# Where the low parts of split activation blocks stand in VectorE's queue

## The chip, the cores and the metric

The kernel runs on one core of a Trainium2 chip. The metric is device time in microseconds (us) of one execution, the median of several runs. A core has TensorE (PE in the profile; its weight loads are shown apart, as PEld), VectorE (DVE), ScalarE (ACT), GpSimd (POOL) and SyncE (SP), each with a queue of its own that is worked off in program order, and 16 DMA engines that the queues feed.

## The reference

One layer of a hybrid decoder for 512 prompt tokens and 8 × 4 new tokens of running sequences, 544 tokens in all, D_MODEL = 2048, float32:

```python
h = rmsnorm(x); proj = h @ w_in                 # q,k,v of 8 heads; q,k,v,gates of 4 GLA heads
gla_part = rmsnorm(gla(...)) * silu(gg)         # gated linear attention, 1024 wide
att_part = rmsnorm(dilated_attention(...))      # 1024 wide
x = x + concatenate([gla_part, att_part]) @ w_out
h = rmsnorm(x)
x = x + square(relu(h @ w_up)) @ w_down         # 4 * D_MODEL wide
y = rmsnorm(x)
```

New keys and values and the states of the linear attention are outputs too.

## The kernel before

**Data.** Activations lie transposed: a tile holds 128 features by 544 tokens, and the matmuls take the tokens in two halves of 272. One core does everything.

**Split operands.** TensorE multiplies in a rounded format (fp32r). So that float32 accuracy is kept, each operand is given as two: a high part, which is the value rounded to fp32r (ACT copies it), and a low part, which is the value minus the high part (DVE subtracts). A product is then three matmuls: high weight × high activation, high × low, low × high. Weights are split by `split_w` (line 231): its high tiles are called wh (whP in the MLP), its low tiles wl (wlP). Activations are split by `put_x` (line 331): ACT writes the high part, and the next instruction that DVE gets is the subtraction that waits for it. Activation tiles are all called b in the profile, whatever they hold, so a DVE row "TENSOR_TENSOR b<-b,b 128x544 fp32r" is the low part of an activation.

**Stages**, in order of time in the profiled execution:

1. Input projection (up to about 720 us), with the attention and the GLA heads worked in between as generators, a step at a time (`bg`). The last of them, `att_norm` (line 663), scales the eight heads of attention (one DVE instruction each, SCALAR_TENSOR_TENSOR with nw) and splits them into the operands Y[0..7].
2. Output projection (about 725 to 927 us), 16 column blocks × two halves of the inner dimension, each a `slot_main` (line 1056) of 48 matmuls. In its first half, `put_go` (line 1126) splits one GLA block per slot, and `state_gen` (line 1224) updates the GLA states of the new tokens (loads and stores on POOL's DMA queue, "b<-vs" and "gs<-b"; DVE adds). In its second half, `evac_wo` (line 1197) puts small pieces of work into a list, `post`: scale the new x, square it, sum, and then form the operands of the MLP (up_b2, up_b1, up_ta, up_ta2, up_tb, up_tb2; `two`, line 1145, and `one` do the splitting).
3. MLP up (about 927 to 1612 us). The product is a 2 × 2 block scheme with seven products (P1 to P7) in place of eight, in 32 pairs of column blocks p = 0..31; a unit is half of one product, 12 matmuls. DVE forms sums of weight quarters (`add_w`) and splits them. What comes out of a pair is evacuated, squared, and mixed again by the pieces of `hidden_ops` (line 1378) into operands for the down product, which are split (`spill_two`, line 1372) and stored to memory ("hs<-b"; for the last four pairs "hl<-b").
4. MLP down (about 1612 us to the end), in seven groups with the operands loaded back ("b<-hs") by `h_some`, then a last group and the final norm.

**What sets the order.** `run` (line 1332) issues a unit: it prepares the weights of the unit three places ahead (ACT high part, DVE sums and low part), then takes one or two pieces from `post`, then issues the 12 matmuls, then the evacuation. `slot_main` does alike: half of the matmuls, one to three pieces from `post`, a step of the generators, the other matmuls. Each engine works its queue in this order.

**Storage.** A tile is taken by `alloc` and given back by `rel`; a slot that was given back is used for a new tile, whose first writer then waits for the last reader of the old one.

Of the kernel before, what the change touches and what calls it, by code (L numbers as in the profile page):

```python
# [6 lines left out]
F32 = mybir.dt.float32  # L7
# [116 lines left out]
def _body(ctx, nc, tc, A):  # L124
# [201 lines left out]
    def mpair():  # L326
        i = mrot[0]
        mrot[0] ^= 1
        return mbank[2 * i], mbank[2 * i + 1]

    def put_x(dst_h, dst_l, src, scale=None):
        if scale is None:
# [330 lines left out]
    def att_norm():  # L663
        ss = None
        for h in range(8):
            while ("p", h) not in att_done or ("s", h) not in att_done:
                yield "wait"
            t = alloc()
            S.activation(t, AO[h], AF.Square)
            if ss is None:  # L670
                ss = t
            else:
                G.tensor_add(ss, ss, t)
                rel(t)
            yield
        while len(bfree) < 2:
            yield "wait"
        b0, b1 = balloc(), balloc()
        r = alloc()
        rms_r(r, [ss], 1024, (b0, b1))  # L680
        brel(b0, b1)
        rel(ss)
        yield
        for h in range(8):
            while room() < 6:
                yield "wait"
            V.scalar_tensor_tensor(AO[h], AO[h], nw[:, 48 + h:49 + h], r, op0=OP.mult, op1=OP.mult)
            a, b = alloc(R32), alloc(R32)
            put_x(a, b, AO[h])
            rel(AO[h])  # L690
            Y[h] = (a, b)
            if h % 2:
                yield
        rel(r)
        att_fin[0] = True

# [359 lines left out]
    def slot_main(i, pb, xs_, c0, first, last, evac=None, nbg=1, hs=(0, 1)):  # L1056
        begin()
        load_to(i + NRAW + 1)
        prep_to(uidx[i] + AHEAD)
        h, l = wops(i)  # L1060
        for q in range(2):
            clk["P"] = max(clk["P"], spl[i, q])
            for c in range(4 * q, 4 * q + 4):
                xh, xl = xs_[c0 + c]
                mm(pb, h(c), xh, first and c == 0, False, hs)
                mm(pb, h(c), xl, False, False, hs)
            for _ in range(1 + (len(post) > 1) + (len(post) > 4)):
                if post:
                    post.pop(0)()
            if q or BG2:  # L1070
                bg(nbg)
            for c in range(4 * q, 4 * q + 4):
                mm(pb, l(c), xs_[c0 + c][0], False, last and c == 7, hs)
            if q == 0:
                prep_to(uidx[i] + AHEAD + 1)
        if evac is not None:
            evac(pb)
        slot[0] += 1
# [46 lines left out]

    def put_go(n):
        a, b = alloc(R32), alloc(R32)
        put_x(a, b, GO[n])
        rel(GO[n])
        Y[8 + n] = (a, b)  # L1130

    xr = {}
# [9 lines left out]
    xa = {}  # L1142
    xtiles = {k: [] for k in ("a2", "ta", "tb", "b1")}

    def two(op, xt, key, src, where):

        h, l = alloc(R32), alloc(R32)
        put_x(h, l, src)
        xtiles[key] += [h, l]
        for hf, k in enumerate(where):  # L1150
            op[k][xt] = (half(h, hf), half(l, hf))

    def one(op, j, src):
        t = alloc(R32)
        put_x(half(t, 0), half(t, 1), src)
        xtiles["b1"].append(t)
        op["P1"][j] = (half(t, 0), half(t, 1))

# [26 lines left out]

    def up_tb2(j):
        tb = mixed.pop((j, 1))
        two(XU, j, "tb", tb, ("P6", "P4"))
        rel(tb)

    def evac_att(nb):
        def f(pb):
# [122 lines left out]
    def product(key, ops, k, blocks, ps, start, stop):  # L1315
        def mm_():
            n = len(blocks)
            for j in blocks:
                while ops[k][j] is None or len(ops[k][j]) < 2:
                    (post if ops is XU else hq).pop(0)()  # L1320
            for w, o in ((whm, 0), (whm, 1), (wlm, 0)):
                for c, j in enumerate(blocks):
                    P.matmul(ps, w[key][:, c, :], ops[k][j][o], start=start and w is whm and o == 0 and c == 0,
                             stop=stop and w is wlm and c == n - 1, skip_group_check=True)
        return mm_
# [6 lines left out]
    def run(us):  # L1332
        for u in us:
            due = [f for s, f in later_u if s <= unit_no[0]]
            later_u[:] = [(s, f) for s, f in later_u if s > unit_no[0]]
            for f in due:
                f()
            prep_to(FIRST + u.step + 3)
            if u.before:
                u.before()  # L1340
            for _ in range(1 + (len(post) > 6)):
                if post:
                    post.pop(0)()
            u.mm()
            if u.after:
                u.after()
            unit_no[0] += 1
# [23 lines left out]

    def spill_two(src, dst, i):
        h, l = alloc(R32), alloc(R32)
        put_x(h, l, src)
        spill(h, dst[i])
        spill(l, dst[i + 1])

    def hidden_ops(p):
        g, j = p // 4, p % 4
        a1, a2 = hid.pop((p, 0)), hid.pop((p, 1))  # L1380
        if g == 7:
            def put(i, a):
                spill_two(a, A["hl"][2 * j + i], 0)
                rel(a)
            post.extend([lambda: V.tensor_mul(a1, a1, rr["sq"]), lambda: V.tensor_mul(a2, a2, rr["sq"]),
                         lambda: put(0, a1), lambda: put(1, a2)])
            return
        dst = A["hs"][g, j]
        m = {}

        def mix_a():
            ta = m["a"] = alloc()
            V.tensor_sub(half(ta, 0), half(a1, 1), half(a1, 0))
            V.tensor_sub(half(ta, 1), half(a1, 1), half(a2, 1))

        def first():
            t = alloc(R32)
            put_x(half(t, 0), half(t, 1), half(a1, 0))
            rel(a1)
            spill(t, dst[6])  # L1400

        def mix_b():
            tb = m["b"] = alloc()
            V.tensor_sub(half(tb, 0), half(a2, 1), half(m["a"], 0))
            V.tensor_sub(half(tb, 1), half(tb, 0), half(a2, 0))

        def put_a():
            spill_two(m["a"], dst, 2)
            rel(m["a"])

        def put_2():
            spill_two(a2, dst, 0)
            rel(a2)

        def put_b():
            spill_two(m["b"], dst, 4)
            rel(m["b"])

        post.extend([mix_a, first, mix_b, put_a, put_2, put_b])

# [348 lines left out]
    for s, (nb, hf) in enumerate(wo_seq):  # L1769
        if s == 16:  # L1770
            drain(lambda: all(n in GO for n in range(8)), gens)
            go_some(8)
            rel(GW["a"], GW["w"])
            for c in range(8):
                rel(*Y[c])
        state_step(2 if s < 16 else 1)
# [61 lines left out]
    for nb in range(16):  # L1838
# [3 lines left out]
        else:  # L1842
            final_out(1, nb)
        out_dma(1, nb, (nc.sync, nc.scalar)[nb % 2])
    assert not later and not later_u and not post


def shape_consts():
# [111 lines left out]
```

## Time and profile before

| | |
|---|---|
| median of 3 runs | 2325.3 us (2323.55 to 2328.4) |
| the profiled execution: its time | 2323.29 us |
| the profiled execution: span from the first to the last instruction | 2321.5 us |
| PE busy | 2277.4 us, 98% of the span |
| DVE busy | 1963.5 us, 85% |
| ACT busy | 1115.3 us, 48% |
| POOL busy | 126.7 us, 5% |
| chain of work that ended last | PE 86%, DVE 7%, DMA 4%, ACT 2% |

All instructions that go through the kernel's helper carry line 96, so groups are told apart by tile and shape. Matmuls are pipelined and their ends are modelled, so "busy" hides short waits; how many matmuls fall into a stretch of time tells more. A bracket behind a row, "[0.72 <-ACT b L96]", is the time that the engine sat idle before it and what ended that. A row that merges several instructions has their number behind an x.

### The profile page before, as it was taken

How to read it: one execution, taken by the hardware profiler on the slowest of the kernel's cores; microseconds unless marked ns; L12 is line 12 of the kernel's file. 1: busy time of each engine (PE TensorE's matmuls, PEld its weight loads, DVE VectorE, ACT ScalarE, POOL GpSimd, SP SyncE). 2: the span in 40 equal slices, each digit the busy share in tenths (PEclk: the TensorE clock that was granted, in tenths of full speed). 3: DMA queues.
4: the chain of work that ended last, by engine and by line, in shares of the span. 5: the costliest groups of instructions: out<-in, count | busy, mean ns of one | idle time of the engine just before them, and what ended most of it. 6: DMA issues, size and time to landing. Idle time of an engine off the chain costs nothing.

```text
span 2321.5 us, 47246 instructions
## 1 busy us (share of the span) xinstructions
PE 2277.4 (98%) x17960; PEld 2247.7 (97%) x17960; DVE 1963.5 (85%) x4343; ACT 1115.3 (48%) x2133; POOL 126.7 (5%) x182
## 2 busy tenths in 40 slices
PE   8999999999999999999999999999999999999997
PEld 8999999999989999999999999999999999999997
DVE  7888877889878987888888888887788888888995
ACT  5333343333345345666666666655444444444465
POOL 3000010000012630000000000000000000000000
PEclk9999999999999999999999999999999999999999
DMA  6777865645735974365566556667755664664564
GB/s 228 265 266 240 287 227 189 219 144 186 242 104 173 349 259 162 112 207 180 186 199 203 177 188 205 197 198 255 266 175 169 217 208 150 217 222 154 170 214 149
DMA packets 168191, 473.43 MB, mean 204 GB/s; under 512 B 20091, under 2 KB 29307, under 8 KB 167964
## 3 DMA queue, kind: packets, MB, share of 16 engines
q1 hardware_dynamic: 157340, 439.67, 56.7%
q0 software_dynamic: 9472, 29.63, 3.6%
q8 instruction: 141, 2.31, 0.4%
q10 hardware_dynamic: 1152, 1.11, 0.1%
q14 instruction: 86, 0.70, 0.1%
HBM read 393.07 MB, written 77.27 MB: 203 GB/s over the span
## 4 chain that ended last, share of the span: by engine, by line
PE 86%; DVE 7%; DMA 4%; ACT 2%; issue 1%; POOL 0%; SPq 0%; DVEq 0%; ACTq 0%
PE bank L96 86%; DVE b L96 5%; DMA b<-vs 2%; ACT b L96 1%; DVE wlP L96 1%; DMA b<-xT 1%; DMA b<-hs 1%; DVE wl L96 1%; ACT whP L96 0%; DMA b<-win 0%; DMA raw<-win 0%; DVE AT L96 0%; ACT wh L96 0%; DVE kv L96 0%; POOL b L96 0%
## 5 line engine op out<-in xcount | busy, mean ns | idle before, releaser
L96 PE MATMUL bank<-b,whP 128*128 128x272 f32 x6720 | 980.4, 288 | 7.5 <-ACT b L96 3.6
L96 PEld LDWEIGHTS bank<-b,whP 128*128 128x128 f32 x6720 | 895.5, 188 | 10.4 <-ACT whP L96 4.4
L96 PE MATMUL bank<-b,wlP 128*128 128x272 f32 x3360 | 561.0, 289 | 2.1 <-DVE wlP L96 2.1
L96 PE MATMUL bank<-b,wh 128*128 128x272 f32 x3904 | 529.9, 288 | 0.3 <-DVE b L96 0.3
L96 PEld LDWEIGHTS bank<-b,wh 128*128 128x128 f32 x3904 | 505.3, 188 | 0.5 <-DVE b L96 0.5
L96 PEld LDWEIGHTS bank<-b,wlP 128*128 128x128 f32 x3360 | 472.9, 188 | 6.6 <-DVE wlP L96 3.4
L96 ACT ACTIVATE whP<-b 128x512 fp32r<-128x512 f32 x480 | 299.3, 627 | 255.7 <-DVE b L96 198.4
L96 ACT ACTIVATE b<-b 128x544 fp32r<-128x544 f32 (+6 forms) x485 | 274.6, 572 | 277.3 <-DVE b L96 245.7
L96 DVE TENSOR_TENSOR wlP<-b,whP 128x512 fp32r<-128x512 f32 x480 | 328.9, 686 | 17.0 <-ACT whP L96 16.5
L96 DVE TENSOR_TENSOR b<-b,b 128x272 f32<-128x272 f32 (+8 forms) x574 | 274.7, 498 | 35.8 <-ACT b L96 31.6
L96 PE MATMUL bank<-b,wl 128*128 128x272 f32 x1952 | 297.8, 295 | 2.7 <-DVE wl L96 2.6
L96 PEld LDWEIGHTS bank<-b,wl 128*128 128x128 f32 x1952 | 261.6, 189 | 9.8 <-issue 4.4
L96 ACT ACTIVATE b<-bank 128x272 f32<-128x272 f32 (+4 forms) x247 | 98.0, 409 | 316.8 <-PE bank L96 293.4
L96 DVE TENSOR_TENSOR b<-b,bank 128x272 f32<-128x272 f32 x388 | 167.3, 433 | 58.4 <-PE bank L96 57.9
L96 DVE TENSOR_TENSOR wl<-raw,wh 128x512 fp32r<-128x512 f32 x244 | 167.0, 692 | 54.7 <-PE bank L96 30.9
L96 ACT ACTIVATE wh<-raw 128x512 fp32r<-128x512 f32 x244 | 149.4, 623 | 128.3 <-PE bank L96 116.0
L96 DVE TENSOR_TENSOR wlP<-mraw,whP 128x512 fp32r<-128x512 f32 x206 | 140.8, 687 | 47.5 <-ACT whP L96 39.1
L96 PE MATMUL bank<-b,b 128*128 128x272 f32 (+5 forms) x968 | 143.1, 304 | 6.3 <-ACT b L96 6.3
L96 ACT ACTIVATE whP<-mraw 128x512 fp32r<-128x512 f32 x206 | 124.0, 621 | 41.4 <-PE bank L96 40.6
L96 POOL TENSOR_TENSOR b<-b,b 128x544 f32<-128x544 f32 (+2 forms) x26 | 36.4, 1403 | 1885.7 <-ACT b L96 1773.3
L96 DVE TENSOR_TENSOR wlP<-raw,whP 128x512 fp32r<-128x512 f32 x154 | 105.4, 687 | 34.5 <-ACT whP L96 28.3
L96 PEld LDWEIGHTS bank<-b,b 128*128 128x128 f32 (+2 forms) x968 | 119.3, 180 | 12.3 <-ACT b L96 6.6
(92 smaller groups left out, 1668.5 us busy)
## 6 DMA issues: line engine op xcount, KB each, us to landing
hs<-b SPq DMA_DIRECT2D x196, 272.0 KB, 6.0
b<-hs SPq DMA_DIRECT2D x196, 272.0 KB, 4.9
raw<-win SPq DMA_DIRECT2D x90, 512.0 KB, 4.2
mraw<-wdn SPq DMA_DIRECT2D x82, 512.0 KB, 3.6
kv<-kcg SPq DMA_DIRECT2D x64, 640.0 KB, 5.3
kv<-vcg SPq DMA_DIRECT2D x64, 640.0 KB, 5.4
mraw<-wup SPq DMA_DIRECT2D x74, 512.0 KB, 4.1
raw<-wdn SPq DMA_DIRECT2D x62, 512.0 KB, 3.7
```

Source lines behind the costliest of these rows:

```text
L96: return f(*a, **k)
```

## The change

A new helper `put_lag` takes the place of `put_x` for the operands of the output projection, of the MLP's first product and of its second. ACT's high part is issued where it was; the DVE subtraction (with the giving back of the source tile) goes into a list `lows`. `flush` issues what is in the list. It is called ahead of each piece taken from `post` (`piece`), ahead of the pieces of a slot and of a unit, in `att_norm` behind the scaling of the next head, at the end of `att_norm` and of the first half of the output projection, and, for the operands of the MLP's first product (tag "X"), ahead of the matmuls of a unit. In the last four pairs of MLP up an empty piece stands ahead of the two splits. The arithmetic is the same.

```diff
+    lows = []
+    def flush(tag=None):
+        for x in [x for x in lows if tag in (None, x[0])]:
+            lows.remove(x)
+            x[1]()
+    def piece():
+        flush()
+        post.pop(0)()
+    def put_lag(tag, dst_h, dst_l, src, *done):
+        S.activation(dst_h, src, AF.Copy)
+        def low():
+            V.tensor_sub(dst_l, src, dst_h.bitcast(F32))
+            rel(*done)
+        lows.append((tag, low))
...
@@ att_norm
             V.scalar_tensor_tensor(AO[h], AO[h], nw[:, 48 + h:49 + h], r, op0=OP.mult, op1=OP.mult)
             a, b = alloc(R32), alloc(R32)
-            put_x(a, b, AO[h])
-            rel(AO[h])
+            flush()
+            put_lag("Y", a, b, AO[h], AO[h])
...
+        flush()
         rel(r)
@@ slot_main
+            flush()
             for _ in range(1 + (len(post) > 1) + (len(post) > 4)):
                 if post:
-                    post.pop(0)()
+                    piece()
@@ put_go
-        put_x(a, b, GO[n])
-        rel(GO[n])
+        put_lag("Y", a, b, GO[n], GO[n])
@@ two (and one alike)
-        put_x(h, l, src)
+        put_lag("X", h, l, src, *done)
@@ product
                 while ops[k][j] is None or len(ops[k][j]) < 2:
-                    (post if ops is XU else hq).pop(0)()
+                    if ops is XU:
+                        piece()
+                    else:
+                        hq.pop(0)()
+            if ops is XU:
+                flush("X")
@@ run
+            flush()
             for _ in range(1 + (len(post) > 6)):
                 if post:
-                    post.pop(0)()
+                    piece()
@@ spill_two (and first alike)
-        put_x(h, l, src)
+        put_lag("H", h, l, src, src)
@@ hidden_ops, g == 7
-            post.extend([lambda: V.tensor_mul(a1, a1, rr["sq"]), lambda: V.tensor_mul(a2, a2, rr["sq"]),
+            post.extend([lambda: V.tensor_mul(a1, a1, rr["sq"]), lambda: V.tensor_mul(a2, a2, rr["sq"]), lambda: None,
                          lambda: put(0, a1), lambda: put(1, a2)])
```

PE's and POOL's queues have the same instructions in the same order before and after. DVE's differ at many places, ACT's and SP's only near the end of MLP up. Three places follow, as they stand in the queues (- before, + after).

DVE, in `att_norm`, heads 0 to 3: each SCALAR_TENSOR_TENSOR scales one head, the TENSOR_TENSOR with two b behind it is that head's low part, and wl is the low part of an input weight.

```order
 L96 SCALAR_TENSOR_TENSOR b_1091<-b_1091,nw,b_8209 128x544
+L96 SCALAR_TENSOR_TENSOR b_1445<-b_1445,nw,b_8209 128x544
 L96 TENSOR_TENSOR b_8311<-b_1091,b_8310 128x544
-L96 SCALAR_TENSOR_TENSOR b_1445<-b_1445,nw,b_8209 128x544
-L96 TENSOR_TENSOR b_8316<-b_1445,b_8315 128x544
-L96 TENSOR_TENSOR wl_0_8330<-raw_8113,wh_0_8277 128x512
+L96 TENSOR_TENSOR wl_0_8329<-raw_8113,wh_0_8277 128x512
+L96 TENSOR_TENSOR b_8315<-b_1445,b_8314 128x544
 L96 SCALAR_TENSOR_TENSOR b_1799<-b_1799,nw,b_8209 128x544
```

The second head's scaling now stands ahead of the first head's low part, and the weight's low part ahead of the second head's.

DVE, in MLP up, pair p = 2, the stretch from the units of P6 to those of P3 and P7: wlP are the low parts of the summed weights (quarters 0 and 1), "b<-mraw,mraw" a weight sum, the TENSOR_TENSOR of 128x544 the low parts of the three mixed blocks of the pair before.

```order
 L96 TENSOR_TENSOR wlP_2_0_11845<-b_11795,whP_2_0_11843 128x512
+L96 TENSOR_TENSOR b_11863<-mraw_11330,mraw_11418 128x512
+L96 TENSOR_TENSOR wlP_2_1_11867<-b_11815,whP_2_1_11865 128x512
 L96 TENSOR_TENSOR b_11848<-b_11776,b_11847 128x544
-L96 TENSOR_TENSOR b_11864<-mraw_11330,mraw_11418 128x512
-L96 TENSOR_TENSOR wlP_2_1_11868<-b_11816,whP_2_1_11866 128x512
+L96 TENSOR_TENSOR wlP_2_0_11893<-b_11841,whP_2_0_11891 128x512
 L96 TENSOR_TENSOR b_11871<-b_11657,b_11870 128x544
-L96 TENSOR_TENSOR wlP_2_0_11894<-b_11841,whP_2_0_11892 128x512
+L96 TENSOR_TENSOR wlP_2_1_11915<-b_11863,whP_2_1_11913 128x512
 L96 TENSOR_TENSOR b_11897<-b_11822,b_11896 128x544
```

Each of the three low parts stands one weight later; the weight of quarter 1 has moved ahead of the first of them.

ACT, in MLP up, pair p = 29, while the two results of pair 28 are split: whP are high parts of weights, "b<-bank" copies out of the accumulators, "b<-b" of 128x544 the high parts of the two results.

```order
 L96 ACTIVATE whP_29_1_19706<-b_19660 128x512
-L96 ACTIVATE b_19710<-b_19385 128x544
-L96 ACTIVATE b_19726<-bank_73 128x272
-L96 ACTIVATE whP_29_0_19734<-b_19685 128x512
-L96 ACTIVATE b_19738<-b_19561 128x544
-L96 ACTIVATE whP_29_1_19756<-b_19704 128x512
+L96 ACTIVATE b_19722<-bank_73 128x272
+L96 ACTIVATE whP_29_0_19730<-b_19685 128x512
+L96 ACTIVATE b_19734<-b_19385 128x544
+L96 ACTIVATE whP_29_1_19751<-b_19704 128x512
+L96 ACTIVATE b_19756<-b_19561 128x544
```

Both high parts stand one unit later, the copy out of the accumulator and the weight of quarter 0 ahead of the first.

More of the change, by code (lines that the diff above doesn't have):

```diff
@@ L1143, in _body, with two @@
     xtiles = {k: [] for k in ("a2", "ta", "tb", "b1")}
-    def two(op, xt, key, src, where):
+    def two(op, xt, key, src, where, *done):
         h, l = alloc(R32), alloc(R32)
-        put_x(h, l, src)
+        put_lag("X", h, l, src, *done)
         xtiles[key] += [h, l]
@@ L1154, in one @@
         t = alloc(R32)
-        put_x(half(t, 0), half(t, 1), src)
+        put_lag("X", half(t, 0), half(t, 1), src)
         xtiles["b1"].append(t)
@@ L1187, in up_tb2 @@
         tb = mixed.pop((j, 1))
-        two(XU, j, "tb", tb, ("P6", "P4"))
-        rel(tb)
+        two(XU, j, "tb", tb, ("P6", "P4"), tb)
     def evac_att(nb):
@@ L1383, in put @@
                 spill_two(a, A["hl"][2 * j + i], 0)
-                rel(a)
-            post.extend([lambda: V.tensor_mul(a1, a1, rr["sq"]), lambda: V.tensor_mul(a2, a2, rr["sq"]),
+            post.extend([lambda: V.tensor_mul(a1, a1, rr["sq"]), lambda: V.tensor_mul(a2, a2, rr["sq"]), lambda: None,
                          lambda: put(0, a1), lambda: put(1, a2)])
@@ L1397, in first @@
             t = alloc(R32)
-            put_x(half(t, 0), half(t, 1), half(a1, 0))
-            rel(a1)
+            put_lag("H", half(t, 0), half(t, 1), half(a1, 0), a1)
             spill(t, dst[6])
@@ L1408, in put_a @@
             spill_two(m["a"], dst, 2)
-            rel(m["a"])
         def put_2():
             spill_two(a2, dst, 0)
-            rel(a2)
         def put_b():
             spill_two(m["b"], dst, 4)
-            rel(m["b"])
         post.extend([mix_a, first, mix_b, put_a, put_2, put_b])
@@ L1773, in _body @@
             rel(GW["a"], GW["w"])
+            flush()
             for c in range(8):
@@ L1844, in _body @@
         out_dma(1, nb, (nc.sync, nc.scalar)[nb % 2])
-    assert not later and not later_u and not post
+    assert not later and not later_u and not post and not lows
 def shape_consts():
```

## Prediction

> **What bounds the kernel now.** I read the page's busy shares first, then the stretches of time, then who waits in those that lose time.
>
> ```profile
> PE 2277.4 (98%) x17960; PEld 2247.7 (97%) x17960; DVE 1963.5 (85%) x4343; ACT 1115.3 (48%) x2133; POOL 126.7 (5%) x182
> PE 86%; DVE 7%; DMA 4%; ACT 2%; issue 1%; POOL 0%; SPq 0%; DVEq 0%; ACTq 0%
> ```
>
> TensorE sets the time: it is 86% of the chain that ended last. DVE is in that chain with 7%, so moving DVE's work can pay only where PE waits. Busy time hides short waits; the number of matmuls in a stretch does not. The view of stretches (span from:to, its length, then busy time with the number of instructions for PE, PEld, DVE, ACT, POOL, then the granted clock, DMA share, GB/s):
>
> ```profile
> 714.00:726.00 12.00, 8.66 (x56) 7.98 (x55) 9.11 (x16) 6.07 (x13) 6.36 (x12) 0.86 0.75 263
> 754.00:780.00 26.00, 26.00 (x210) 26.00 (x209) 25.14 (x54) 10.33 (x20) 16.73 (x32) 1.00 0.96 347
> 780.00:816.00 36.00, 33.33 (x258) 32.23 (x257) 31.26 (x66) 10.31 (x20) 21.70 (x41) 1.00 0.97 353
> 924.00:936.00 12.00, 8.41 (x57) 8.22 (x56) 8.45 (x16) 6.75 (x12) 1.08 (x2) 0.86 0.12 48
> 968.00:992.00 24.00, 22.66 (x174) 21.85 (x172) 22.39 (x44) 14.21 (x29) 0.00 (x0) 1.00 0.52 168
> 992.00:1552.00 560.00, 559.98 (x4439) 556.79 (x4440) 491.96 (x870) 353.54 (x687) 0.00 (x0) 1.00 0.61 194
> 1552.00:1612.00 60.00, 57.24 (x441) 55.26 (x440) 48.58 (x80) 33.14 (x64) 0.00 (x0) 1.00 0.67 219
> 1612.00:1626.00 14.00, 12.17 (x93) 11.61 (x93) 11.09 (x19) 8.57 (x17) 0.00 (x0) 1.00 0.98 367
> 1626.00:2146.00 520.00, 520.00 (x4153) 520.00 (x4154) 452.09 (x861) 220.44 (x377) 0.00 (x0) 1.00 0.59 197
> ```
>
> MLP down (1626:2146) runs without waits: 520/4153 = 0.1252 us per matmul. By that price the others lose: 714:726 5.0 us (12 − 56 × 0.1252); 780:816 3.7; 924:936 4.9; 968:992 2.2; 992:1552 4.2; 1552:1612 4.8; 1612:1626 2.4. The change can reach at most about these 27 us, 1.2% of the time. I go through them in order.
>
> **A, 714:726, the split of the attention heads.** From the timeline (start, length, engine):
>
> ```profile
> 704.47 0.78 DVE L96 SCALAR_TENSOR_TENSOR b<-b,nw,b 128x544 f32<-128x544 f32 x1
> 705.28 0.66 ACT L96 ACTIVATE b<-b 128x544 fp32r<-128x544 f32 x1 [5.01 <-DVE b L96]
> 705.97 0.73 DVE L96 TENSOR_TENSOR b<-b,b 128x544 fp32r<-128x544 f32 x1 [0.72 <-ACT b L96]
> 709.43 0.78 DVE L96 SCALAR_TENSOR_TENSOR b<-b,nw,b 128x544 f32<-128x544 f32 x1
> 713.02 0.61 ACT L96 ACTIVATE wh<-raw 128x512 fp32r<-128x512 f32 x1
> 719.98 0.72 DVE L96 TENSOR_TENSOR b<-b,b 128x544 f32<-128x544 f32 x1
> 720.75 2.18 PE L96 MATMUL bank<-b,ones 128*128 128x272 f32 x4 [3.34 <-DVE b L96]
> ```
>
> For each head DVE scales, stands idle 0.72 us for ACT's high part, and subtracts. Three pairs of heads stand ahead of the sum at 719.98 that the matmul with ones waits for, and PE sits idle 3.34 us. A pair takes 709.43 − 704.47 = 4.96 us. In the new order the second scaling fills the first wait, and the second high part runs under the first low part. What is left is the weight's low part, which waits for the weight's high part, on ACT behind the second head's (0.66 + 0.61 us, less the low part's 0.64 beside it, as from 1032.44 to the next start at 1033.08 in C's rows: about 0.6 idle). The pair then takes 0.75 + 0.75 + 0.03 + 0.64 + 0.6 + 0.6 + 0.64 = 4.0 us, 0.95 less. Two pairs give 1.9 us; in the third, two evacuations stand between, cover both waits and give 0.7. That is 2.6 of PE's 3.34 us, the rest stays. Bounds: 0.7 (only the third pair pays, if the weights wait for PE) and 3.34.
>
> The row has a second price: the granted clock is 0.86 over these 12 us. At half clock that is 3.4 us, and of these PE works some 2.6 (from 720.75), which costs 1.3 us. A wait of 0.7 us in place of 3.3 should not bring that on. [...] A gives 2.6 + 1.3 = **3.9 us**, between 0.7 and 4.6.
>
> Does it come through? In 754:816 the DMA engines are 96 to 97% busy with the GLA states, and a chain of loads leads there:
>
> ```profile
> 742.26 0.16 DVE b L96
> 753.99 7.62 DMA b<-vs
> 805.85 5.70 DMA b<-vs
> ```
>
> The chain begins behind a DVE evacuation at 742.26, which itself waits for PE, and the DMA share of 714:726 is 0.75. So that work starts earlier by as much as PE does, and the stretch moves as a whole. Inside it DVE has 25.14 us of work in 26, no wait for ACT to remove. I take 0 for it; bounds −1 and +1 (one weight per slot comes a low part's 0.6 us earlier; or DMA meets other traffic).
>
> **B, 924:936, the first block of MLP up.**
>
> ```profile
> 924.32 0.69 DVE L96 TENSOR_TENSOR wlP<-mraw,whP 128x512 fp32r<-128x512 f32 x1 [0.34 <-issue]
> 926.79 0.73 DVE L96 TENSOR_TENSOR b<-b,b 128x544 fp32r<-128x544 f32 x1 [0.73 <-ACT b L96]
> 931.12 0.73 DVE L96 TENSOR_TENSOR b<-b,b 128x544 fp32r<-128x544 f32 x1 [0.72 <-ACT b L96]
> 931.76 0.78 DVE L96 TENSOR_TENSOR b<-bank,b 128x272 f32<-128x272 f32 x2
> 932.31 0.95 PEld L96 LDWEIGHTS bank<-b,whP 128*128 128x128 f32 x4 [3.78 <-ACT b L96]
> ```
>
> PE's wait of 3.78 us ends as the evacuation at 931.76 frees the bank. Of the two waits ahead of it the second stays: three pieces are taken in that slot, so its low part falls back in front of the evacuation. The first (0.73) goes, but a low part that stood ahead of 924.32 now stands behind that weight, which waits anyway (0.34, "issue"), and adds its 0.64. I take **0.1 us**, between −0.6 and 1.4 (the half clock gone too). **968:992** is a chain of evacuations, activations and weights, in which one low part moves behind the evacuation that ACT waits for; of 2.2 us I take a low part's 0.64, **0.6 us**, between 0 and 1.5.
>
> **C, 992:1552, the steady part of MLP up.** A pair of blocks is 14 units of 12 matmuls, 168; 4439/168 = 26.4 pairs, so 4.2 us are 0.16 us per pair. The timeline shows it, once per pair:
>
> ```profile
> 1032.44 0.72 DVE L96 TENSOR_TENSOR b<-b,b 128x544 fp32r<-128x544 f32 x1
> 1033.08 0.69 DVE L96 TENSOR_TENSOR b<-mraw,raw 128x512 f32<-128x512 f32 x1
> 1033.68 0.69 DVE L96 TENSOR_TENSOR wlP<-b,whP 128x512 fp32r<-128x512 f32 x1
> 1032.74 0.56 PEld L96 LDWEIGHTS bank<-b,wlP 128*128 128x128 f32 x4
> 1033.24 1.06 PEld L96 LDWEIGHTS bank<-b,whP 128*128 128x128 f32 x8
> 1034.42 0.55 PEld L96 LDWEIGHTS bank<-b,wlP 128*128 128x128 f32 x4
> ```
>
> A load of wlP should follow that of whP by 1.0 us; here it is 1.18, because DVE ends the weight at 1034.37. The low part at 1032.44 is the instruction that moves behind it. So the weight ends 0.64 earlier, 0.46 before PE asks. The two weights after it also have one low part less ahead of them, and the evacuation at the end has all three ahead as before. The removed wait does not come back elsewhere: DVE works 491.96 of 560 us. The stores of the low parts keep their place on SP, three units behind, 4.5 us against a low part that is up to 1.3 us later. All of it: **4.2 us**; bounds 0 (the weight waits for something else) and 4.8 (26.4 × 0.18).
>
> **D, 1552:1612, the last three pairs.**
>
> ```profile
> 1561.87 0.68 DVE L96 TENSOR_TENSOR wlP<-b,whP 128x512 fp32r<-128x512 f32 x1
> 1562.58 0.66 ACT L96 ACTIVATE b<-b 128x544 fp32r<-128x544 f32 x1 [2.73 <-DVE wlP L96]
> 1563.15 0.61 ACT L96 ACTIVATE whP<-b 128x512 fp32r<-128x512 f32 x1
> 1563.27 0.73 DVE L96 TENSOR_TENSOR b<-b,b 128x544 fp32r<-128x544 f32 x1 [0.72 <-ACT b L96]
> 1563.81 1.05 PEld L96 LDWEIGHTS bank<-b,whP 128*128 128x128 f32 x8 [0.64 <-ACT whP L96]
> 1565.38 0.55 PEld L96 LDWEIGHTS bank<-b,wlP 128*128 128x128 f32 x4 [0.52 <-DVE wlP L96]
> ```
>
> A high part waits on ACT for the DVE weight that reads the slot it will take; the next weight's high part is stuck behind it (PE waits 0.64), then DVE waits for ACT ahead of that weight's low part (0.52). In the new order the low part ahead of 1561.87 is gone from there, so the weight, the ACT high part and the weight behind it come about 0.65 earlier, and the second low part stands behind the next weight: both waits of PE should go, and its wait for the unit after should stay in part. Of 1.6 us per pair I take 0.87, for three pairs **2.6 us**, between 0 and 4.3.
>
> **1612:1626** is a wait for operands loaded back, two waves of loads:
>
> ```profile
> 1612.88 6.08 DMA b<-hs
> 1619.03 6.07 DMA b<-hs
> ```
>
> They are released by PE, which ends the last pair; the number of loads ahead of and behind that point is the same in the new order. I take 0, between −3 and +0.5.
>
> **The sum.** 3.9 + 0 + 0.1 + 0.6 + 4.2 + 2.6 + 0 = 11.4 us. The profiled execution took 2323.3 us (span 2321.5), 2.0 under the median of the three runs and 0.3 under the lowest of them. I set the level at 2324.4, the middle of these four values, and forecast **2313 us**.
>
> **Rivals.**
>
> 1. *The DMA stretch eats A.* If the states' loads cannot start earlier, 754:816 ends where it does now and A is lost: 2324.4 − 7.5 = 2316.9. For it: 96 to 97% DMA share. Against it: the share ahead of it, and the chain that starts at DVE. Chance 0.15.
> 2. *The waits move to ACT.* DVE no longer waits, but each weight needs its high part, and ACT has the same queue; if whP is what PE really waits for in C and D, only A and B's part are left: 2324.4 − 4.6 = 2319.8. For it: in D PE is already put down to ACT whP. Against it: in C the weight's DVE instruction starts at once behind the sum, without a wait for ACT. Chance 0.13.
> 3. *Late low parts hold SP back* (slower). The stores of low parts wait for DVE in SP's queue, and weight loads stand behind them. If a store waits for its low part, a weight load starts later by up to 0.64 us in each of 26.4 pairs: 17 us, less A, B and D (7.2): 2324.4 + 9.7 = 2334. It decides from the point where a weight arrives less than 0.64 us before ACT asks for it. Against it: the three units of distance; and the view of waits for MLP up names no wait of ACT for a weight load. Chance 0.06.
> 4. *B keeps its clock.* 924:936 has granted clock 0.86 too, 3.4 us at half, of which PE works 2.6: 1.3 us. Idle stretches of 3.34 (A) and 3.78 us (B) brought that on; if B's, 0.1 shorter and at another moment, does not, it is 2311.7. No row tells how it will fall. [...] Chance 0.06.
>
> The forecast has 0.60. Ends of the range: with all upper bounds the gain would be 18 us (2306), which needs all of them at once; I set 2307. The upper end takes in rivals 1 and 2 and a little more: 2321. What a measurement here tells from no change is about 0.2%, 4.7 us: rival 2 stands at that edge. Faster by more than that: 0.60 + 0.15 + 0.06 + a third of 0.13, 0.85; within it 0.09; slower 0.06.
>
> **What would show it.** PE's 3.34 us ahead of the matmul with ones shrinks under 1.5, and the clock there reads 1.00 (A). In 560 us of MLP up there are about 4470 matmuls, and the load of wlP follows whP by 1.0 us throughout (C). In the last three pairs PE's waits for whP behind a high part go (D). B's 3.78 us stays above 3. It is wrong if the stretch from 754 grows by what A gains, if PE's waits are named ACT whP instead of DVE wlP, or if SP's stores wait for DVE.

## The result, and the profile after

The changed kernel takes 2309.8 us (median of 6 runs, 2308.15 to 2312.0), the kernel before 2326.1 us in the same session (6 runs, 2323.55 to 2328.4): a ratio of 0.9927 (95% interval 0.9915 to 0.9938), 16.3 us less. The forecast was 2313 us, 11.4 us less than the level that it set out from. The profiled execution took 2309.52 us, span 2307.7, which is 13.8 us under the span of the profile before.

The page of the changed kernel, busy shares and chain:

```profile
PE 2270.5 (98%) x17960; PEld 2246.6 (97%) x17960; DVE 1962.6 (85%) x4343; ACT 1116.0 (48%) x2133; POOL 126.1 (5%) x182
PE 85%; DVE 7%; DMA 3%; ACT 2%; issue 2%; SPq 0%; POOL 0%; DVEq 0%; ACTq 0%
```

The shares tell nothing: DVE does the same work. The stretches do. Since the order of the matmuls is the same in both kernels, a stretch can be cut at the same two matmuls in each, and its length compared. The view of stretches of the kernel before, cut so (columns as in the prediction):

```profile
716.50:734.40 17.90, 14.56 (x103) 13.88 (x102) 15.04 (x29) 11.79 (x20) 3.85 (x8) 0.90 0.77 273
772.07:828.94 56.87, 54.20 (x423) 52.98 (x422) 51.07 (x108) 18.16 (x37) 35.67 (x67) 1.00 0.98 357
969.80:992.38 22.58, 21.22 (x162) 20.41 (x161) 20.97 (x41) 13.41 (x28) 0.00 (x0) 1.00 0.48 158
992.38:1552.47 560.09, 560.09 (x4443) 556.90 (x4441) 492.05 (x871) 353.49 (x687) 0.00 (x0) 1.00 0.61 195
1552.47:1594.18 41.71, 39.41 (x302) 37.87 (x301) 32.74 (x54) 23.00 (x44) 0.00 (x0) 1.00 0.64 212
1594.18:1611.45 17.27, 16.81 (x133) 16.37 (x131) 14.82 (x25) 9.71 (x20) 0.00 (x0) 1.00 0.73 234
1611.45:1626.56 15.11, 13.28 (x101) 12.72 (x102) 11.68 (x20) 9.54 (x19) 0.00 (x0) 1.00 0.98 359
```

and of the changed kernel, between the same matmuls:

```profile
716.50:729.48 12.98, 12.98 (x103) 12.82 (x102) 11.09 (x22) 9.64 (x16) 3.31 (x7) 1.00 0.90 316
767.14:820.71 53.57, 53.29 (x423) 52.84 (x422) 50.62 (x108) 17.61 (x33) 33.71 (x64) 1.00 1.00 373
961.53:983.15 21.62, 21.02 (x163) 20.43 (x162) 20.64 (x41) 13.54 (x28) 0.00 (x0) 1.00 0.50 170
983.15:1542.29 559.14, 556.90 (x4443) 555.61 (x4442) 492.92 (x871) 353.22 (x687) 0.00 (x0) 1.00 0.59 195
1542.29:1579.83 37.54, 37.54 (x302) 37.54 (x301) 31.36 (x53) 22.54 (x44) 0.00 (x0) 1.00 0.66 220
1579.83:1597.63 17.80, 16.52 (x133) 16.33 (x132) 14.49 (x24) 9.22 (x19) 0.00 (x0) 1.00 0.70 227
1597.63:1613.75 16.12, 14.25 (x103) 14.06 (x102) 11.69 (x21) 8.76 (x18) 0.00 (x0) 0.89 0.96 359
```

The wait ahead of the sum of the heads (A) is gone altogether: 4.9 us. The DMA stretch, forecast at 0, is 3.3 us shorter. The last pairs (D), 1552:1611, are 58.98 us before and 55.34 after. The steady MLP up (C), forecast at 4.2, gives only 0.95: in the row before, PE is busy all of the time and a little slow; in the row after, 2.2 us of idle have come in. The wait that the prediction had found is gone; its place in the changed kernel (start, length, engine):

```profile
1023.86 1.06 PEld L96 LDWEIGHTS bank<-b,whP 128*128 128x128 f32 x8
1024.85 0.56 PEld L96 LDWEIGHTS bank<-b,wlP 128*128 128x128 f32 x4
```

The load of wlP follows that of whP by 0.99 us, where it took 1.18. In each of the five profiles below with the MLP in the old order, one matmul at this place starts 0.1 us late in all of 26 pairs; in the nine others none does. The view of waits says what came instead. Kernel before, 992.38:1552.47 (engine and tile, what it waited for, us in total, times, longest):

```profile
ACT b L96 <- DMA hs<-b: 14.2, 25, 0.7
```

Changed kernel, 983.15:1542.29:

```profile
ACT b L96 <- DMA hs<-b: 22.1, 27, 2.3
PEld bank L96 <- ACT whP L96: 3.5, 6, 0.8
PE bank L96 <- ACT whP L96: 2.2, 6, 0.5
```

In this pair of profiles ACT's high part waits longer for a store out of the slot that it is to fill, up to 2.3 us instead of 0.7, and in six places a weight's high part on ACT comes too late for PE. In three of them it stands right behind the high part that waited. The chain of one of these (start, length, what) and ACT's timeline there:

```profile
1148.63 5.11 DMA hs<-b
1153.77 0.03 ACT b L96
...
1154.34 0.62 ACT whP L96
```

```profile
1153.77 0.66 ACT L96 ACTIVATE b<-b 128x544 fp32r<-128x544 f32 x1 [2.16 <-DMA hs<-b]
1154.34 0.61 ACT L96 ACTIVATE whP<-b 128x512 fp32r<-128x512 f32 x1
```

The stalls that PE has in the steady part of the changed kernel's first profile are 0.71, 0.49, 0.57, 0.49, 0.43 and 0.49 us, by the late starts of its matmuls. Each 0.49 comes two units behind the stall before it: DVE is late there, and at 1156.69 ACT's activations wait 1.22 us for it, with the next weights' high parts behind them.

### The profile page after: what moved, and what is told of

It is laid out like the page before. It is cut to its first block, busy times and chain, and to the rows that moved or that the text cites. A ratio compares the mean times of both kernels' runs of the same rounds, so it can differ in the third digit from the quotient of the medians.

```text
span 2307.7 us, 47242 instructions
## 1 busy us (share of the span) xinstructions
PE 2270.5 (98%) x17960; PEld 2246.6 (97%) x17960; DVE 1962.6 (85%) x4343; ACT 1116.0 (48%) x2133; POOL 126.1 (5%) x182
## 4 chain that ended last, share of the span: by engine, by line
PE 85%; DVE 7%; DMA 3%; ACT 2%; issue 2%; SPq 0%; POOL 0%; DVEq 0%; ACTq 0%
PE bank L96 85%; DVE b L96 6%; ACT b L96 1%; DVE wlP L96 1%; DVE wl L96 1%; DMA hs<-b 1%; DMA b<-xT 1%; ACT whP L96 1%; DMA b<-vs 0%; DMA raw<-wout 0%; DMA b<-win 0%; DMA hl<-b 0%; ACT wh L96 0%; DMA raw<-win 0%; DMA b<-wglr 0%
```

## The experiments

Lengths in us between the same matmuls, in every profile taken (the columns named by the times of the kernel before; worked out from the start times of the matmuls in each trace):

| run | A 716.5:734.4 | DMA 772:829 | 970:992 | C 992:1552 | D 1552:1611 | 1611:1627 | MLP down |
|---|---|---|---|---|---|---|---|
| before | 17.90 | 56.87 | 22.58 | 560.09 | 58.98 | 15.11 | 679.87 |
| before, again | 19.34 | 56.56 | 22.56 | 560.35 | 58.98 | 15.21 | 679.87 |
| before, third | 18.06 | 57.02 | 22.57 | 562.19 | 58.97 | 15.44 | 679.86 |
| changed | 12.97 | 53.57 | 21.61 | 559.15 | 55.34 | 16.12 | 678.92 |
| changed, again | 12.97 | 55.42 | 21.59 | 558.52 | 55.23 | 16.12 | 678.88 |
| changed, third | 12.97 | 54.19 | 21.57 | 559.08 | 55.62 | 14.58 | 678.87 |
| heads only | 12.97 | 53.90 | 22.57 | 562.13 | 58.97 | 15.57 | 679.65 |
| heads and GLA blocks only | 12.97 | 55.18 | 22.57 | 563.11 | 58.99 | 15.48 | 680.33 |
| second product's operands only | 18.94 | 55.10 | 21.61 | 559.25 | 55.01 | 14.66 | 680.11 |
| changed, no empty piece | 12.97 | 54.73 | 21.59 | 559.16 | 57.16 | 15.90 | 680.06 |
| changed, last pairs direct | 12.97 | 53.88 | 21.57 | 559.57 | 58.94 | 15.16 | 680.64 |
| changed, stores at 2 units | 12.97 | 54.05 | 21.59 | 555.06 | 54.72 | 16.96 | 680.47 |
| the same, again | 12.97 | 53.66 | 21.60 | 555.05 | 54.62 | 16.82 | 680.45 |
| changed, stores at 2 units by GpSimd | 12.97 | 58.38 | 21.59 | 555.65 | 55.52 | 15.86 | 680.56 |

The matmul at 716.5 us, ahead of which no edit reaches PE, comes at 716.4 to 719.8 us in these profiles. So the difference of two single profiles is not the effect of an edit; a difference in one column that comes out alike each time is.

**The heads alone.** In `put_lag` only the tag "Y" is held back, the GLA blocks have another tag, and the empty piece is left out:

```diff
+        if tag in ('Y',):
+            lows.append((tag, low))
+        else:
+            low()
...
-        put_lag("Y", a, b, GO[n], GO[n])
+        put_lag("Z", a, b, GO[n], GO[n])
```

> Only the eight attention heads are split with the low part held back (in att_norm); every other low part stands directly behind its high part, and there is no empty piece. Question: the change made 714:726 shorter by 4.9 us and, unforeseen, 754:816 by 3.3 us. Theory: the DMA stretch 754:816 gained because the chain of state loads that leads into it started earlier, so it comes with the heads: gain 4.9 + 3.3 = 8.2 us, ratio 0.9965 (about 2318). Rival: the 3.3 us come from the GLA blocks, whose low parts no longer stand ahead of the next weight inside that stretch: gain 4.9 us alone, ratio 0.998 (about 2321), and PE stalls about 3.7 us in 780:816 as before. A second rival: the DMA stretch is bound by its transfers and gives A back: ratio 1.000.

Measured: 2322.3 us, ratio 0.9983 (0.9968 to 0.9998). The wait in A is gone with this part alone, and the DMA stretch is 53.90 us, so the GLA blocks are not needed for that. The time alone would have spoken for the rival (0.998); the stretches do not. But C took 562.13 us, with the MLP in the old order: two stalls of 1.0 us, with the same chain as in the changed kernel. Chain of this run:

```profile
1149.88 5.94 DMA hs<-b
...
1155.84 0.03 ACT b L96
...
1156.41 0.62 ACT whP L96
```

The wait for the store is therefore not a child of the change alone. The old order has it too, and how much PE loses by it differs between executions.

**Heads and GLA blocks.** As above, but the GLA blocks keep the tag "Y" and are held back too.

> The attention heads and the GLA blocks are split with the low part held back, the MLP is as before. By both readings of 754:816 this holds the whole gain up to 900 us: 4.9 + 3.3 = 8.2 us, ratio 0.9965 (about 2318), and the MLP up takes as long as in the kernel before. If it is much more than that, part of what the whole change gained in MLP up comes from the earlier arrival there and not from the order in MLP up; if the GLA blocks cost something (their low parts come later than the loads want them), it is less than the run with the heads alone.

Measured: 2322.7 us, ratio 0.9985 (0.9973 to 0.9997). The GLA blocks bring nothing that can be told (DMA stretch 55.18 against 53.90); C took 563.11, again with stalls behind hs stores. Neither run reached the 8.2 us of its theory in time: the medians are 4.2 and 3.8 us lower, though A and the DMA stretch of their profiles gave 7.9 and 6.6. C took 2 to 3 us more than in the first profile of the kernel before, which the repeats below put in its place.

**The second product's operands alone.** Only the tag "H" is held back, with the empty piece.

> Only the operands of the second product (hidden_ops, with the empty piece) are split with the low part held back. Theory: 992:1552 gains only about 1 us, because the stall of 0.17 us per pair is replaced by waits of ACT's high part for the store of the slot that it takes; 1552:1612 gains 3.6, 1612:1626 loses 1.0, together 3.6 us: ratio 0.9985 (about 2322), and the view of waits of 992:1552 shows ACT b behind DMA hs<-b with some 21 us and waits of up to 2 us, as in the changed kernel. Rival: those waits come from where the whole change puts MLP up in time (its phase against the DMA); then here 992:1552 gains the forecast 4.2, together some 6.8 us, ratio 0.997, and ACT's waits for hs<-b stay at some 14 us and under 0.8 us.

Measured: 2319.4 us, ratio 0.9968 (0.9956 to 0.9981), 7.2 us. C 559.25, D 55.01, and the 1 us of 970:992, which I had put down to an order in that stretch without saying whose: it belongs to this part, since both runs without it have 22.57. No run holds back the first product's operands (tag "X") alone; no stretch shows a gain that would be left for them. The stalls of 0.3 to 0.6 us behind ACT's wait for hs<-b are there (the row reads 20.6 us in all, 2.2 longest, in 985:1545), so they do not come from the earlier arrival: the theory holds on the wait. On the time its 3.6 us were too few, and the rival's 6.8 nearer: against the mean of the old order C gains 2.4 us (561.6 to 559.25), D 4.0 and 970:992 1.0. And with nothing changed up to 900 us, the DMA stretch was 55.10, 1.8 us less than in the kernel before.

**Without the empty piece.**

```diff
-...V.tensor_mul(a2, a2, rr["sq"]), lambda: None,
+...V.tensor_mul(a2, a2, rr["sq"]),
```

> The changed kernel without the empty piece in the last four pairs of MLP up. There the two splits are then issued one piece earlier. Theory: the new stall of 1.5 us in the last pairs of the changed kernel and the 2.0 us at their end are waits for stores of slots (hl<-b) that the empty piece makes later; without it 1552:1626 is shorter by 1 to 2.5 us: ratio to the kernel before 0.992 (about 2308). Rival: the empty piece is what takes the splits out of the way of the weights, and without it the last pairs lose some 2 to 4 us of their gain: ratio 0.9945 (about 2312.5).

Measured: 2314.0 us, ratio 0.9942 (0.9925 to 0.9959). D is 57.16 in place of 55.23 to 55.62, and stalls of 0.3 to 0.8 us are back. The rival was right in kind, its 2 to 4 us a little high: the empty piece is worth 1.5 to 1.9 us in the last pairs. The new stall (1.4 us, now 0.42) did fall, as the theory had it, but that pays less.

**Before and after again.** A second and a third profile of each.

> The kernel before once more, to see how far a stretch differs between two executions of the same program. In the profile of before PE lost 3.3 us in 754:816 (stalls of 0.80, 0.80, 1.14 and 0.56 us); the runs with one part of the change lost 0.3 to 0.6 there in the same matmuls (one of them 1.9 just behind), among them the run with the MLP's low parts alone, in which nothing is changed up to 900 us. Theory: the 3.3 us in the DMA stretch are the lot of one execution, and this one shows another number, between 0.3 and 3.3 (a gain that the change did not make). Rival: they belong to the old order, and the stalls come back at the same matmuls with 3 us in all. All other stretches (714:726 with 3.5 us of idle, the steady MLP up without a stall over 0.3 us, the last pairs, the 1.0 and 1.2 us at 1614 and 1624) should come back within 0.3 us by either.

> The changed kernel once more, on the chip on which the two versions with earlier stores run. Theory: the stalls of 0.4 to 0.7 us in 992:1552 come back at about the same matmuls (in the pairs in which a high part takes the slot of the operand that is stored alone), 2 to 4 us in all, with the two of 1.4 and 2.0 us at the end of MLP up; time 2308 to 2314, ratio to before 0.993. Rival: they were the lot of that one execution, and most of them are gone.

> The kernel before a third time, for two things that differed between executions of one program. [...] Second the DMA stretch 754:816: old order so far 3.3, 2.9 and 1.3 us of stalls, new order 0.3 to 4.0. Theory: by lot, so anything from 0.5 to 4; if it is again near 3, the old order is worse there by some 1.5 us on the mean.

> The changed kernel a third time, as the partner of the version with earlier stores on the same chip: ratio to before 0.993, with 2.5 to 4 us of stalls in 992:1552, of 1.3 to 1.5 and 2.0 us at the end of MLP up, and no half clock ahead of the output projection's second quarter (714:726 at 1.00).

Measured: the kernel before 2324.97 and 2327.42 us, one run each; the changed kernel 2312.4 us, ratio 0.9932 (0.9916 to 0.9948), and 2311.6 us, ratio 0.9942 (0.9928 to 0.9956). In the changed kernel the stalls of 0.4 to 0.7 us came back at about the same matmuls, so they are no lot of one execution. For the kernel before three things follow. C went from 560.09 to 560.35 and 562.19, so its first profile, on which the prediction was built, was a lucky one there, and "no stall over 0.3 us" was wrong as a property of the old order. ACT's wait for the stores is longer in the repeats, too. The second profile, 985:1545, and two rows of the third, 994.11:1556.30:

```profile
ACT b L96 <- DMA hs<-b: 17.3, 26, 1.4
```

```profile
ACT b L96 <- DMA hs<-b: 19.7, 26, 2.0
PEld bank L96 <- ACT whP L96: 1.9, 3, 1.0
```

So most of the step from 14.2 to 22.1 us, and all but 0.3 us of that from 0.7 to 2.3, is within what the old order does by itself. A had 17.90, 19.34 and 18.06, and 18.94 in the run with the second product's operands: the stall is 3.3 to 3.5 us each time, but the half clock behind it cost 1.0 and 1.4 us more in two of the four (granted clock 0.83 and 0.89 in 712:724 and 724:736 of the second profile, 0.94 and 0.77 with the second product's operands, against 0.86 and 1.00 in the first), against the expectation that this stretch comes back within 0.3 us. The DMA stretch, in all profiles with the heads in the old order, took 55.1 to 57.0 us (mean 56.4, four profiles), in those with the heads in the new order 53.6 to 58.4 (mean 54.7, ten). The theory that it is all by lot is too strong, and the rival that it belongs to the order is not shown either: the ranges overlap.

**Stores one unit earlier.**

```diff
             nc.sync.dma_start(dst, t.bitcast(F32))
             rel(t)
-        defer_u(3, f)
+        defer_u(2, f)
```

> The changed kernel with the operands of the second product stored two units behind their split rather than three. The lone store of a pair then stands on SP ahead of the weight load that waits some 9 us for DVE, and not behind it. Theory: the stalls left in 992:1552 of the changed kernel (3.2 us with their after-effects some 3.7) and those of 1.4 and 2.0 us at the end of MLP up are ACT's high part waiting for such a store; the store lands 1.5 us or more earlier and they go: 4 to 6 us less than the changed kernel, ratio to before about 0.991. ACT's wait for hs<-b falls from 21.4 us to under 14. Rival: the stores now wait on SP for the low part, which is written in the unit before, and hold the weight loads behind them: ACT whP or DVE waits for mraw appear, and the time is that of the changed kernel or 1 to 10 us more.

> The changed kernel with the second product's operands stored two units behind their split, once more with more rounds. Its 992:1552 was 3.5 us shorter than the changed kernel's, with no wait for a store left, while the medians differed by 1.8 us with an uncertainty of the same size. Theory: 992:1552 and the time are 3 to 4 us under the changed kernel's, ratio to before 0.9915. Rival: the earlier stores cost elsewhere what they save there (the stretch behind MLP up), and the two medians agree within 1 us.

Measured: 2310.6 us, ratio 0.9924 (0.9910 to 0.9939), beside 2312.4 for the changed kernel; again 2309.7, ratio 0.9928 (0.9915 to 0.9941), beside 2311.6. The steady part of the second run, in the view of stretches:

```profile
985.22:1540.26 555.04, 555.04 (x4443) 555.04 (x4442) 491.92 (x871) 352.59 (x686) 0.00 (x0) 1.00 0.62 196
```

PE and its weight loads are busy in every moment of 555 us; no row of its view of waits names hs<-b or lets PE wait. That is 5.0 us under the first profile of the kernel before: all of C's forecast, and more. But the reason that I had written down, that the store is ahead of a weight load on SP and so lands earlier, is wrong. The lone store of a pair went out 0.50 us behind the start of the DVE group that holds its low part in both. SP and DVE of the changed kernel:

```profile
1148.13 1.27 DVE L96 TENSOR_TENSOR b<-b,b 128x272 fp32r<-128x272 f32 x3
1148.63 0.33 SPq L1395 DMA_DIRECT2D hs<-b  x1
```

and of the version with earlier stores:

```profile
1148.72 1.26 DVE L96 TENSOR_TENSOR b<-b,b 128x272 fp32r<-128x272 f32 x3
1149.22 0.32 SPq L1395 DMA_DIRECT2D hs<-b  x1
...
1152.42 0.66 ACT L96 ACTIVATE b<-b 128x544 fp32r<-128x544 f32 x1 [0.22 <-DVE wlP L96]
```

What differs is the slot. A slot is given back at the place in the program where its store is issued; one unit earlier, the last high part of a pair gets a slot whose store has long landed. The order of the built programs tells which: ACT's row with the semaphores that it waits for, and behind it the last store on that DMA semaphore. In the changed kernel, and with the same tiles in the kernel before:

```
L96 ACTIVATE b590_12480<-b581_12406 128x544 [waits DMAHW5_49]
L1395 DMA hs<-b579_12385 128x544 [waits DMAHW5_49,DVE_49,Activation_49]
```

That is the lone store of the same pair. In the version with earlier stores it is one of the pair before:

```
L96 ACTIVATE b590_12482<-b581_12406 128x544 [waits DMAHW1_49,DVE_49]
L1395 DMA hs<-b568_12190 128x544 [waits DMAHW1_49,Activation_49]
```

On the time, the theories of 4 to 6 and of 3 to 4 us and the second run's rival (within 1 us) were all off: 1.8 and 1.9 us less, and the intervals of the two versions overlap, so that it is faster is likely and not shown. The table has where the rest went: C gains 3.5 to 4.1 us, D 0.5 to 1.0, but 1611:1627 and MLP down lose 0.7 to 2.4 and some 1.6, and what stands behind MLP down's column 0.8 to 1.1. Why those stretches lose was not looked at.

**The same stores by GpSimd.** `nc.gpsimd` in place of `nc.sync` there, two units behind.

> The changed kernel with those stores issued by GpSimd's queue, which has nothing else to do in MLP up, two units behind the split. There they neither wait for a weight load nor hold one. Theory (slots wait for stores that stand behind weight loads on SP): as with the earlier stores on SP, 4 to 6 us less than the changed kernel, ratio about 0.991, and the waits of SP for DVE in 992:1552 stay on weight loads alone. Rival 1: it is the landing of the store (5 to 6 us) and not its place in the queue that decides; then the stalls stay as they are, ratio 0.993. Rival 2: a store issued by GpSimd lands later (GpSimd issues one in 0.54 us, the row of gs<-b) or slows DVE; then slower than the changed kernel.

Measured: 2312.3 us, ratio 0.9926 (0.9908 to 0.9944). The 4 to 6 us of the theory did not come: the time is that of the changed kernel. In the profile the DMA stretch, far ahead of these stores, took 58.38 us, 4 us more than in its sisters. C is 555.65, within 0.6 us of the other version: with the slots alike, it hardly matters which queue issues the stores. That supports the slot, and speaks against the place on SP and against rival 1, by which the stalls would have stayed.

**The last pairs direct.** `put_x` in place of `spill_two`'s `put_lag` for the last four pairs, and no empty piece.

> The changed kernel with the last four pairs of MLP up split as before (low part directly behind the high part, no empty piece). Theory: the gain in 1552:1612 comes from these low parts being held back; PE's waits of 0.3 to 0.8 us per pair (some 4.3 us in three pairs) come back, the new stalls of 1.4 and 2.0 us at the end go or fall to the 1.0 and 1.2 us of before, and 1552:1626 is 2.5 us longer than in the changed kernel: about 2313 to 2315. Rival: the new stalls at the end cost as much as the waits that went, and the stretch is as long as in the changed kernel within 0.7 us.

Measured: 2315.8 us, one run. D is 58.94, as in the kernel before, and PE's waits of 0.3 to 0.8 us are back at the same matmuls. The stalls behind are back to 1.00 and 1.23 us. Taken together, 1552:1627 is 74.10 us, against 71.46, 71.35 and 70.20 in the changed kernel: 2.6 to 3.9 us, the theory's 2.5 or more. The time is a little above its 2313 to 2315, with one run alone.

## Why the prediction came out as it did

The time lay 3 us under the forecast. The steps that looked for DVE's waits held; C was too high, and A, the DMA stretch and D too low. "The mean" below is over all profiles with the old or the new order in that stretch.

- **A, forecast 3.9 us (0.7 to 4.6): 4.93 against the first profile, and 5.6 against the mean of four profiles in the old order** (18.56 − 12.97). The mechanism is right, one sub-step is wrong. I let the weight's low part wait some 0.6 us for its high part in each pair. DVE's timeline after:

```profile
704.47 1.47 DVE L96 SCALAR_TENSOR_TENSOR b<-b,nw,b 128x544 f32<-128x544 f32 x2
705.97 0.73 DVE L96 TENSOR_TENSOR b<-b,b 128x544 fp32r<-128x544 f32 x1
706.62 0.69 DVE L96 TENSOR_TENSOR wl<-raw,wh 128x512 fp32r<-128x512 f32 x1
707.22 0.72 DVE L96 TENSOR_TENSOR b<-b,b 128x544 fp32r<-128x544 f32 x1
707.85 1.48 DVE L96 SCALAR_TENSOR_TENSOR b<-b,nw,b 128x544 f32<-128x544 f32 x2
```

There is no idle: the pair takes 3.38 us (707.85 − 704.47) and not 4.0. ACT's timeline has a weight's high part at 706.54, only 0.08 us ahead of this low part, so the low part at 706.62 is that of an earlier one, whose high part was there; I had paired the two that stand side by side. PE's whole 3.3 us went, and the half clock with it (granted clock 0.90 between these matmuls before, 1.00 after). That a wait of 0.7 us would leave the clock alone was my estimate, and no run shows it: none left such a wait there.

- **754:816, forecast 0 (−1 to 1): 3.3 us in the first pair of profiles, and outside my bounds.** By the means it is 1.7 us (56.4 to 54.7), and single profiles differ by as much as 4.8 us in the new order. The term was mis-sized, or rather given bounds that a single profile cannot give. Rival 1 (the stretch eats A) is refuted in nine of the ten profiles with the heads in the new order; in the tenth, 58.38 against 56.87, it ate 1.5 us of A. The tenth, that of the stores by GpSimd, has a stall of 2.4 us there. Why the stretch is shorter on the mean I cannot say: its chain is held by loads b<-vs in profiles of both orders (93.1% in 780:816 of the kernel before, 90.5% in the second profile of the changed one), and in the first of the changed kernel by DVE's own work (52.5%, b<-vs 11.5%).

- **B, forecast 0.1:** the first block stayed within 0.1 us, but 0.07 the other way (from 927.84 to 936.34 us before, from 919.42 to 927.99 after, by the starts of its matmuls), and its stall at 3.57 us, above 3, as forecast; the half clock stayed (granted clock 0.80 between these matmuls in both). **968:992, forecast 0.6: 0.97**, the same in every profile with that part. The mechanism is as told: with one low part behind the evacuation the stall at 977.8 fell from 1.19 to 0.52 us, a low part's length. Most of the rest is the first of C's late matmuls, which stands at the end of this stretch.

- **C, forecast 4.2 (0 to 4.8): 0.95 in the first pair of profiles, 2.6 by the means** (561.6 in five profiles with the MLP in the old order, 558.9 in three of the changed kernel). The removed wait was rightly named: the late load of wlP is gone in every pair, and with the store waits gone too the gain is 5.0 us, 0.19 per pair. The step that failed is "The removed wait does not come back elsewhere: DVE works 491.96 of 560 us". It looked at DVE's load alone. ACT's waits for hs<-b stood in the view of waits of the kernel before, 25 of them in the same stretch, and were not read. One high part in each pair takes a slot whose store is still landing, and waits up to 0.7 us for it in that profile, up to 2.1 in others of the same order. That is how 3.5 to 4.1 us of the 5.0 came back in the changed kernel (558.5 to 559.2 against 555.04). The old order lost 0 to 3 us to it as well, so about 2.4 us of it, on the mean, came with the change. Whether by stores that go out later, or since PE now comes earlier, no run tells. So rival 2 came true in part: in C, PE waits for ACT whP, which I had named as a sign that I am wrong. Rival 3 (SP's queue held by late low parts) did not, though its sign was there: in 992:1552 SP's stores waited for a b that DVE writes 33 times, 22.4 us in all, against 14 times, 11.1 us, before. But no engine's wait for a weight load appears in the view, and the run with GpSimd's queue has C within 0.6 us of that with SP's.

- **D, forecast 2.6 (0 to 4.3): 3.4 to 3.8 us**, from the last pairs' low parts alone, as the run with these direct shows. In 1552:1594 every one of the seven waits went, 4.2 us, near the upper bound of 4.3, where I took 60% because I let PE's wait for the unit after stay in part; it went whole. A new wait behind it takes 0.4 to 0.8 back: DVE's evacuation waits for a slot that an hl store still reads.

```profile
1582.43 0.44 DVE L96 TENSOR_TENSOR b<-bank,b 128x272 f32<-128x272 f32 x1 [2.06 <-DMA hl<-b]
```

- **1612:1626, forecast 0 (−3 to 0.5): 1.0 us lost, twice, and 0.5 won, once.** PE's idle there is 2.0 us in one piece instead of 1.0 and 1.2 in two, and the clock goes with the sign: 0.89 with 1.0 us lost in the first profile, 1.00 with 0.5 won in the third. The reading as a wait for loads was half right: by the views of waits one of the two was for DVE (0.9 us) and one for b<-hs (1.0); after, it is DVE alone, up to 1.9 us. With the last pairs direct the two are back, so the longer wait comes from their held-back low parts.

Against the profiled spans the sum is 4.93 + 3.30 + 0.97 + 0.95 + 3.64 − 1.01 + 0.95 (MLP down) = 13.7 us of 13.8. The medians differ by 16.3, which is 2.5 more. The first profile of the kernel before was short in A (by 0.7 us against the mean) and in C (by 1.5), which would make 2.2 of it. That the forecast's total of 11.4 was near is therefore partly luck: against the mean C was 1.6 too high, and A 1.7, the DMA stretch 1.7 and D 1.0 too low.

MLP down, where nothing is changed, is 1.0 us shorter in all three profiles of the changed kernel and 0.2 to 0.8 longer in most of the versions. No cause was looked for.

## What to carry to other kernels

Before an engine's wait is removed, read which waits of the other engines end just ahead of PE's need, down to those of 0.5 us: they are next, and one that stands there 25 times in a stretch may be the next limit. When the wait is for a slot, look at which slot is taken and where in the program it is given back; here one unit in that place was worth 3.5 to 4 us of that stretch (though less than 2 of the whole time), and the queue that issued the store 0.6 at most. And one profile is one draw: here a stretch with DMA at 97% and more came out up to 4.8 us apart in profiles with the same order of the heads, and a wait of 2.00 us had half clock behind it in some profiles and not in others. Such a stretch needs two or three profiles before a few microseconds in it mean anything.

## What the runs showed of the hardware that was not expected

The same wait of PE brings half clock in one execution and not in the next. In the changed kernel PE waits 2.00 us for DVE ahead of a matmul with ones, in each profile. The first, PE's timeline and the stretch:

```profile
693.57 0.70 PE L96 MATMUL bank<-b,ones 128*128 128x272 f32 x2 [2.00 <-DVE b L96]
```

```profile
688.00:700.00 12.00, 10.00 (x84) 8.80 (x83) 8.21 (x29) 7.35 (x14) 1.35 (x1) 1.00 0.16 48
```

and the third profile of the same kernel:

```profile
694.93 1.19 PE L96 MATMUL bank<-b,ones 128*128 128x272 f32 x2 [2.00 <-DVE b L96]
```

```profile
688.00:700.00 12.00, 10.00 (x72) 8.65 (x71) 7.38 (x27) 6.87 (x14) 1.69 (x1) 0.86 0.15 48
```

84 matmuls at full clock, 72 at 0.86, and 1.5 us lost. Of eleven profiles, whose programs are the same up to there, four have 0.86 in this stretch (the second and the third of the changed kernel, that with the second product's operands alone, the first with the stores at 2 units) and seven have 1.00. At some 1.5 us of idle near 669 us there were both too (0.86 in 664:676 behind 1.51 us in the first profile of the changed kernel, 1.00 behind 1.50 us in the kernel before), and near 1601, where PE is busy 10.13 and 10.14 us of 12 (0.86 in 1600:1612 of the first profile of the changed kernel, where PE sat idle 1.87 us in one piece, 1.00 in 1602:1614 of the third).

The first profiles of the two kernels have low clock in five places ahead of their last matmuls, at 1.51, 1.87, 3.34, 3.41 and 3.59 us of PE's idle time. In stretches of 1 us it reads 0.50 in the middle of each, and the five sum up to 3.40 to 3.42 us at half clock each. In the second profile of the kernel before the two stretches from 712 to 736 us, 0.83 and 0.89, make 6.7 us. So the length of the idle time does not tell alone: 2.01 us in the kernel before and 2.00 in the changed kernel left the clock at 1.00, 1.51 and 1.87 us in the changed kernel did not. Rival 4, that no row tells how the clock will fall, was right in that, at other places than B.

A store of 272 KB took 5.11 and 5.94 us to land in the two chains above, in the changed kernel and in the one with the heads alone. The later landing stands with the longer stall, 1.02 against 0.57 us, though in that run no low part of the second product was held back.
